# A two-layer convolution trunk on one core: each silu as one table function, the GLU's sigmoid from a tanh

## The chip, the cores and the metric

One core of a Trainium2 chip runs the kernel. Its engines work side by side, each through its own queue in order: TensorE (PE in the profile; PEld is its weight load), VectorE (DVE), ScalarE (ACT), GpSimd (POOL) and SyncE (SP), whose queue issues all transfers here. An engine that waits at an instruction holds up everything behind it in its queue. The metric is the device time of one execution in microseconds (us); lower is better.

## The reference, cut to what matters

Input x is 2048 tokens by 1024 channels in float32. Two mixers, each followed by a residual and a layer norm:

```python
cond = silu(c)                                 # scales, shifts and gates come from products with it
# layer 0 (mixer A)
a, g, z = split(u @ w_in + b_in, 3)
h = a * sigmoid(g)                             # the GLU
h = causal_depthwise_conv_31(h) + conv_b
h = silu(layer_norm_channels(h, ln_g, ln_b))
y = (h * silu(z)) @ w_out + b_out
# layer 1 (mixer B)
B, C, v, z = split(u @ w_in, 4)
y = (B * conv_3(C * v) * silu(z)) @ w_out
# both: u = x * (1 + scale) + shift;  x = layer_norm(alpha * x + gate * y)
```

silu(t) is t times sigmoid(t), and sigmoid(t) equals 0.5 * tanh(t / 2) + 0.5.

## The kernel before

Tokens go in four quarters q of 512, channels in eight blocks e of 128. A tile of 128x512 holds one block of channels (partitions) for one quarter. Every float32 operand of a product is split in a high part (a cast on ScalarE, L118 and L150) and a low part (a subtraction, mostly on GpSimd, L120 and L151), and a product is three matmuls: high with high, high with low, low with high. One output block of an input product is 24 matmuls (8 blocks of u, three each).

In layer A, `a_in` makes blocks a, g, z for each e (tiles `pi`, one PSUM bank each). `gated_a` (L446 to L451) copies a with its bias to `av`, makes `sg`, the sigmoid of g, and GpSimd multiplies them to `h`. `conv_a` then runs 31 taps in two chains, `pca` and `pcb`, which VectorE adds up (L409); ScalarE starts them (L397 `pcb`, L398 `acc`). There are two PSUM banks for the chains, so that `pcb` of block e can start only when block e-1 is done. `silu_z_a` copies z to `zv`, makes `sz`, its sigmoid, and GpSimd multiplies them (L458 to L461); the result goes to DRAM and comes back later as `zz`, in two buffers.

`a_norm` brings the conv's outputs `acc` to norm: for each e two VectorE rows with the broadcast statistics (L546, L547), then on ScalarE `v` (the scaled and shifted value, L550) and `sv` (its sigmoid, L552), then on VectorE v*sv (L555) and v*zz (L556), then the split to `ga` (cast on ScalarE, low part on GpSimd). `mixer_out` multiplies `ga` by W_out (tiles `wo`, loaded in pairs of blocks, two raw buffers) into four banks `po`, one per 128 tokens, for two halves of the output channels.

In layer B, `gated_b` takes the four blocks `pq`; for z it makes the sigmoid `szb` (L606, ScalarE) and multiplies it by z, read from its PSUM bank, on VectorE (L607). The banks of `pi`, `pq` and `po` come from one pool of four (tag mm), so a `po` bank is the bank of an earlier `pi` or `pq`, and comes free when the last reader of that is done.

`prep` loads blocks of x (`xk`, two buffers), transposes them on TensorE into `ptx` and makes `u`.

The program is written as generators that are woven together by a table of numbers (`SCH`); the order in each engine's queue is then set by a list scheduler with a timing model of its own. Any change of an instruction can thus move others in all queues.

Of the kernel before, what the change touches and what calls it, by code (L numbers as in the profile page):

```python
# [9 lines left out]
F32 = mybir.dt.float32  # L10
F32R = mybir.dt.float32r
AF = mybir.ActivationFunctionType
ALU = mybir.AluOpType
# [3 lines left out]
P = 128  # L17
# [21 lines left out]
def hybrid_trunk(ctx, tc, x, c, ada_w, ada_b, a_w_in, a_b_in, a_conv_w, a_conv_b,  # L39
# [16 lines left out]
    # ------------------------------------------------------------ constants  # L56
# [48 lines left out]
    nc.scalar.activation(cond, col["c"], AF.Sigmoid)  # L105
    nc.vector.tensor_tensor(cond, cond, col["c"], op=ALU.mult)
# [5 lines left out]
    # ------------------------------------------------------------ helpers  # L112
    def weight(src, name, tags=MAIN):
        """A piece of a weight matrix as two float32r parts."""
# [15 lines left out]
    def products(pss, ws, acts):  # L130
        """One or more output blocks, the shared activations outermost."""
# [30 lines left out]
    def prep_k(q, l, k, src, su, bu, tag="xk"):  # L162
        """One block of channels of u, transposed, as two parts."""
# [26 lines left out]
    def ada_sum(l, m, h, res, shared=0):  # L190
        """Products of the condition with half a chunk of ada_w, not yet summed over partitions.

        The last shared ones are summed apart, by other engines.
        """
# [29 lines left out]
    def modulation_b():  # L224
        """Scale and bias of u of the second layer, its input being the first one's bare norm."""
# [21 lines left out]
    def fold_gate(l, w_out, scaled=None):  # L247
        """W_out with the gate of its output channels (over alpha); scaled is a row to take it too."""
# [27 lines left out]
    def mixer_out(q, l, gs, residual, finish, last=False):  # L276
        """r = residual + gated output product, rows in token order, then the norm."""
# [52 lines left out]
    # ------------------------------------------------------------ layer A  # L330
# [50 lines left out]
    in_order[0] = False  # L381
    todo = deque()
# [3 lines left out]
    def conv_a(q, e, h, accs):  # L386
        """Queues two interleaved chains of taps, so that no step waits for the one before it."""
# [55 lines left out]
    def gated_a(q, e, pa, pg, accs):  # L443
        bias = lambda m: col["b_in"][:, m * K + e:m * K + e + 1]
        av = st("ta", [P, T], f"av{q}_{e}")
        nc.scalar.activation(av, pa, AF.Identity, bias=bias(0))  # L446
        sg = st("ta", [P, T], f"sg{q}_{e}")
        nc.scalar.activation(sg, pg, AF.Sigmoid, bias=bias(1))
# [6 lines left out]
    def silu_z_a(q, e, pz):  # L455
        bz = col["b_in"][:, 2 * K + e:2 * K + e + 1]
        zv = st("ta", [P, T], f"zv{q}_{e}")
        nc.scalar.activation(zv, pz, AF.Identity, bias=bz)  # L458
        sz = st("ta", [P, T], f"sz{q}_{e}")
        nc.scalar.activation(sz, pz, AF.Sigmoid, bias=bz)  # L460
        nc.gpsimd.tensor_tensor(zv, zv, sz, op=ALU.mult)  # L461
        nc.sync.dma_start(z_dram[q, e], zv)
# [273 lines left out]
```

## Time and profile before

| What | Value |
|---|---|
| Median of 3 runs | 1782.88 us (1782.02 to 1783.66) |
| Profiled execution: span from first to last instruction | 1780.3 us (no other time of it is listed) |
| PE, DVE, POOL, ACT busy | 94%, 78%, 65%, 37% of the span |
| Mean granted TensorE clock | 0.978 of full speed |

The span is 2.6 us under the median; this is taken as what lies around it. Busy shares are means over stages with different limits.

### The profile page before, as it was taken

What the parts mean: (1) busy time and instruction counts of PE and PEld (TensorE: products, weight loads), DVE (VectorE), ACT (ScalarE), POOL (GpSimd) and SP (SyncE); (2) the same over time, 40 slices, a digit from 0 to 9 for tenths busy, and PEclk for the clock granted to TensorE, in tenths of its full rate; (3) what the DMA queues carried; (4) which work ended last, traced back from release to release, by engine and by line L of the source; (5) the groups of instructions that cost most, each with busy time, mean ns of one, the idle gap of its engine ahead of it and who ended that gap; (6) DMA issues with size and microseconds to landing.
All of it is one profiled execution on the core that took longest, in us unless ns stands there. A gap on an engine that the chain in (4) does not pass through costs nothing.

```text
span 1780.3 us, 20731 instructions
## 1 busy us (share of the span) xinstructions
PE 1675.2 (94%) x7468; PEld 1373.0 (77%) x7468; DVE 1383.5 (78%) x1811; ACT 654.4 (37%) x852; POOL 1157.2 (65%) x742
## 2 busy tenths in 40 slices
PE   6997998899999999999999799999999979999997
PEld 4775787678787787888888687888888868888886
DVE  7999999999996846899995926499996756354464
ACT  2443535545221543344422433243432424222221
POOL 3696857887665867766654857666654666664444
PEclk9998999899999999999999899999999989999999
DMA  9874334676653454533433454443333335443342
GB/s 250 269 242 154 101 118 154 227 229 201 219 176 103 152 191 164 182 114 107 116 87 94 142 166 172 160 130 113 90 107 103 133 107 201 128 144 95 95 142 83
DMA packets 332055, 265.29 MB, mean 149 GB/s; under 512 B 10536, under 2 KB 289456, under 8 KB 331952
## 3 DMA queue, kind: packets, MB, share of 16 engines
q1 hardware_dynamic: 331952, 263.96, 47.3%
q8 instruction: 59, 0.97, 0.2%
q14 instruction: 44, 0.36, 0.1%
HBM read 230.36 MB, written 33.55 MB: 148 GB/s over the span
## 4 chain that ended last, share of the span: by engine, by line
PE 62%; DVE 24%; issue 5%; POOL 4%; DMA 3%; SPq 1%; ACT 1%; POOLq 0%; DVEq 0%; ACTq 0%
PE pq L141 8%; PE pq L139 8%; PE pq L140 8%; PE pi L140 7%; PE pi L141 7%; PE pi L139 7%; DVE pca L409 5%; PE po L311 5%; PE po L313 5%; PE po L312 5%; DVE pcb L409 4%; DVE cc L611 2%; DVE ada L219 1%; DVE v L555 1%; POOL wb_lo L120 1%
## 5 line engine op out<-in xcount | busy, mean ns | idle before, releaser
L120 POOL TENSOR_TENSOR wb_lo<-wb_raw,wb_hi 128x1024 fp32r<-128x1024 f32 x128 | 311.6, 2437 | 213.6 <-ACT wb_hi L118 184.7
L409 DVE SCALAR_TENSOR_TENSOR pca<-h,cols,pca 128x512 f32<-128x512 f32 x440 | 328.3, 746 | 1.3
L409 DVE SCALAR_TENSOR_TENSOR pcb<-h,cols,pcb 128x512 f32<-128x512 f32 x416 | 310.3, 746 | 22.4 <-ACT pcb L397 22.2
L120 POOL TENSOR_TENSOR wi_lo<-wi_raw,wi_hi 128x1024 fp32r<-128x1024 f32 x96 | 234.3, 2442 | 133.8 <-ACT wi_hi L118 121.0
L118 ACT CAST wb_hi<-wb_raw 128x1024 fp32r<-128x1024 f32 x128 | 134.4, 1051 | 365.6 <-PE pq L140 176.8
L120 POOL TENSOR_TENSOR wo_lo<-wo_raw,wo_hi 128x1024 fp32r<-128x1024 f32 (+1 forms) x65 | 164.8, 2538 | 77.2 <-ACT wo_hi L118 59.7
L118 ACT CAST wi_hi<-wi_raw 128x1024 fp32r<-128x1024 f32 x96 | 100.6, 1048 | 211.1 <-PE pi L140 105.6
L320 DVE TENSOR_TENSOR r<-po,r 128x512 f32<-128x512 f32 x64 | 43.3, 681 | 169.8 <-PE po L313 169.6
L118 ACT CAST wo_hi<-wo_raw 128x1024 fp32r<-128x1024 f32 (+1 forms) x65 | 67.0, 1033 | 117.3 <-PE po L313 62.2
L611 DVE SCALAR_TENSOR_TENSOR cc<-hb,cols,cc 128x512 f32<-128x512 f32 x64 | 87.2, 1363 | 0.8
L602 DVE TENSOR_TENSOR hb<-pq,cv 128x512 f32<-128x512 f32 x32 | 22.0, 686 | 68.6 <-PE pq L141 65.1
L409 DVE SCALAR_TENSOR_TENSOR pca<-h,cols,acc 128x512 f32<-128x512 f32 x32 | 51.7, 1617 | 2.4 <-ACT acc L398 2.4
L141 PE MATMUL pq<-u_0h,wb_lo 128*128 128x512 f32 x128 | 50.7, 396 | 1.9 <-POOL wb_lo L120 1.9
L139 PE MATMUL pq<-u_0h,wb_hi 128*128 128x512 f32 x128 | 50.7, 396 | 1.6 <-ACT wb_hi L118 1.6
L139 PE MATMUL pi<-u_0h,wi_hi 128*128 128x512 f32 x96 | 39.2, 409 | 13.8 <-ACT wi_hi L118 12.6
L613 DVE TENSOR_TENSOR cc<-cc,szb 128x512 f32<-128x512 f32 x32 | 51.5, 1608 | 0.5
L141 PE MATMUL pq<-u_2h,wb_lo 128*128 128x512 f32 x128 | 50.9, 398 | 0.0
L140 PE MATMUL pq<-u_4l,wb_hi 128*128 128x512 f32 x128 | 50.3, 393 | 0.0
L140 PE MATMUL pq<-u_6l,wb_hi 128*128 128x512 f32 x128 | 50.2, 392 | 0.0
L140 PE MATMUL pq<-u_0l,wb_hi 128*128 128x512 f32 x128 | 50.2, 392 | 0.0
L140 PE MATMUL pq<-u_7l,wb_hi 128*128 128x512 f32 x128 | 50.1, 392 | 0.0
L141 PE MATMUL pq<-u_4h,wb_lo 128*128 128x512 f32 x128 | 50.1, 392 | 0.0
(376 smaller groups left out, 5228.8 us busy)
## 6 DMA issues: line engine op xcount, KB each, us to landing
wb_raw<-in_b_w_in_dram SPq DMA_DIRECT2D x128, 512.0 KB
wi_raw<-in_a_w_in_dram SPq DMA_DIRECT2D x96, 512.0 KB
wo_raw<-w_dram SPq DMA_DIRECT2D x63, 512.0 KB
adaw<-in_ada_w_dram SPq DMA_DIRECT2D x60, 256.0 KB
adak<-in_ada_w_dram SPq DMA_DIRECT2D x32, 256.0 KB
xk<-in_x_dram SPq DMA_DIRECT2D x32, 256.0 KB
z_dram<-zv SPq DMA_DIRECT2D x32, 256.0 KB
zz<-z_dram SPq DMA_DIRECT2D x32, 256.0 KB
```

Source lines behind the costliest of these rows:

```text
L118: nc.scalar.copy(hi, raw)
L120: nc.gpsimd.tensor_tensor(lo, raw, hi.bitcast(F32), op=ALU.subtract)
L139: nc.tensor.matmul(ps, hi[k], ah, start=(k == 0), stop=False)
L140: nc.tensor.matmul(ps, hi[k], al, start=False, stop=False)
L141: mm = nc.tensor.matmul(ps, lo[k], ah, start=False, stop=(k == K - 1))
L311: nc.tensor.matmul(pss[t], gh[:, sl], hi, start=(k == 0), stop=False)
L312: nc.tensor.matmul(pss[t], gh[:, sl], lo, start=False, stop=False)
L313: nc.tensor.matmul(pss[t], gl[:, sl], hi, start=False, stop=(k == K - 1))
L320: nc.vector.tensor_tensor(r, pss[t], r, op=ALU.add)
L409: nc.vector.scalar_tensor_tensor(out=ts[dst], in0=h[:, k:k + T], scalar=wa_col(k, e), in1=ts[src], op0=ALU.mult, op1=ALU.add)
L611: nc.vector.scalar_tensor_tensor(out=cc, in0=hb[:, k:k + T], scalar=wbc(k), in1=cc, op0=ALU.mult, op1=ALU.add)
L613: nc.vector.tensor_tensor(cc, cc, sz, op=ALU.mult)
```

## The change

Every silu becomes one ScalarE instruction with the function Silu: for the condition, for z of layer A, after layer A's norm, and for z of layer B. Three copies-or-sigmoids per place become one, and the products go: 32 on GpSimd (L461), 64 and one small one on VectorE (L555, L607, L106). In the GLU the sigmoid becomes a tanh with scale 0.5 and a halved bias, and one more ScalarE instruction, `sg*0.5 + 0.5`. Two small constants are added. ScalarE's queue holds one table load, at the condition's function, before and after; in the changed queue Silu and Tanh follow each other 56 times.

```diff
-    nc.scalar.activation(cond, col["c"], AF.Sigmoid)
-    nc.vector.tensor_tensor(cond, cond, col["c"], op=ALU.mult)
+    nc.scalar.activation(cond, col["c"], AF.Silu)
...
+    half_bg = const.tile([P, K], F32, name="half_bg")
+    nc.vector.tensor_scalar(half_bg, col["b_in"][:, K:2 * K], 0.5, None, op0=ALU.mult)
+    half_col = const.tile([P, 1], F32, name="half_col")
+    nc.vector.memset(half_col, 0.5)
...
         sg = st("ta", [P, T], f"sg{q}_{e}")
-        nc.scalar.activation(sg, pg, AF.Sigmoid, bias=bias(1))
+        nc.scalar.activation(sg, pg, AF.Tanh, scale=0.5, bias=half_bg[:, e:e + 1])
+        nc.scalar.activation(sg, sg, AF.Identity, scale=0.5, bias=half_col)
...
-        nc.scalar.activation(zv, pz, AF.Identity, bias=bz)
-        sz = st("ta", [P, T], f"sz{q}_{e}")
-        nc.scalar.activation(sz, pz, AF.Sigmoid, bias=bz)
-        nc.gpsimd.tensor_tensor(zv, zv, sz, op=ALU.mult)
+        nc.scalar.activation(zv, pz, AF.Silu, bias=bz)
         nc.sync.dma_start(z_dram[q, e], zv)
...
-            nc.scalar.activation(v, pt, AF.Identity, scale=g_, bias=b_)
-            sv = st("tv", [P, T], f"sv{q}_{e}")
-            nc.scalar.activation(sv, pt, AF.Sigmoid, scale=g_, bias=b_)
+            nc.scalar.activation(v, pt, AF.Silu, scale=g_, bias=b_)
             zz = st("zz", [P, T], f"zz{q}_{e}")
             nc.sync.dma_start(zz, z_dram[q, e])
-            nc.vector.tensor_tensor(v, v, sv, op=ALU.mult)
             nc.vector.tensor_tensor(v, v, zz, op=ALU.mult)
...
-        nc.scalar.activation(sz, pss[2], AF.Sigmoid)
-        nc.vector.tensor_tensor(sz, pss[2], sz, op=ALU.mult)
+        nc.scalar.activation(sz, pss[2], AF.Silu)
```

The queues change in order too. In the rows below the first number behind a tile's name is the block e (for `wi` and `pi` e and which of a, g, z), and for `xk`, `ptx` and `u` the quarter and the block; a trailing longer number is only the program's count of tiles. The line numbers of the changed kernel are one lower up to the GLU, and a few higher behind it.

ScalarE, first quarter of layer A, around the start of block 3's chain `pcb`, before:

```order
L118 CAST wi_5_2_hi<-wi_5_2_raw 128x1024
L397 ACTIVATE pcb_3_1128<-h_3_1030,cols_397 128x512
L446 ACTIVATE av_5_1315<-pi_5_0_1248,cols_199 128x512
L118 CAST wi_6_0_hi<-wi_6_0_raw 128x1024
L448 ACTIVATE sg_5_1317<-pi_5_1_1290,cols_199 128x512
L118 CAST wi_6_1_hi<-wi_6_1_raw 128x1024
```

The same place of the same queue in the changed kernel:

```order
L117 CAST wi_6_0_hi<-wi_6_0_raw 128x1024
L449 ACTIVATE av_5_1308<-pi_5_0_1241,cols_198 128x512
L400 ACTIVATE pcb_3_1123<-h_3_1028,cols_396 128x512
L117 CAST wi_6_1_hi<-wi_6_1_raw 128x1024
L452 ACTIVATE sg_5_1310<-pi_5_1_1283,half_bg 128x512
L453 ACTIVATE sg_5_1310<-sg_5_1310,half_col 128x512
```

The cast of the weights of block 6's a now stands ahead of `pcb` of block 3, where it stood behind it.

ScalarE, norm of the third quarter (the second in which `po` follows blocks `pq` of layer B), around the sigmoid `szb` of block 6, before:

```order
L150 CAST ga_4h<-v_4_8103 128x512
L552 ACTIVATE sv_6_8133<-acc_6_7233,cols_199 128x512
L118 CAST wo_2_0_4_hi<-wo_2_0_4_raw 128x1024
L150 CAST ga_5h<-v_5_8117 128x512
L606 ACTIVATE szb_6_8331<-pq_6_3_8306 128x512
L550 ACTIVATE v_7_8145<-acc_7_7304,cols_199 128x512
L150 CAST ga_6h<-v_6_8131 128x512
L552 ACTIVATE sv_7_8147<-acc_7_7304,cols_199 128x512
L150 CAST ga_7h<-v_7_8145 128x512
```

The same place in the changed kernel:

```order
L149 CAST ga_5h<-v_5_7996 128x512
L552 ACTIVATE v_7_8018<-acc_7_7202,cols_198 128x512
L149 CAST ga_6h<-v_6_8007 128x512
L149 CAST ga_7h<-v_7_8018 128x512
L117 CAST wo_2_0_4_hi<-wo_2_0_4_raw 128x1024
L149 CAST gb_5h<-cc_5_8060 128x512
L605 ACTIVATE szb_6_8200<-pq_6_3_8175 128x512
```

`szb` of block 6, now the silu and the last reader of its bank, stands behind the casts of the whole norm, where the sigmoid stood behind `ga_5h`.

TensorE, first quarter of layer A, where the first blocks of the second quarter are transposed, before:

```order
L139 MATMUL pi_3_1_1001<-u_0_0h,wi_3_1_hi 128x512
L140 MATMUL pi_3_1_1001<-u_0_0l,wi_3_1_hi 128x512
L169 MATMUL ptx_1_0_1668<-ident,xk_1_0_1666 128x128 x4
L169 MATMUL ptx_1_1_1681<-ident,xk_1_1_1679 128x128
L141 MATMUL pi_3_0_959<-u_0_0h,wi_3_0_lo 128x512
```

TensorE in the changed kernel, at the end of that quarter:

```order
L138 MATMUL pi_7_2_1618<-u_0_7h,wi_7_2_hi 128x512
L139 MATMUL pi_7_2_1618<-u_0_7l,wi_7_2_hi 128x512
L140 MATMUL pi_7_2_1618<-u_0_7h,wi_7_2_lo 128x512
L168 MATMUL ptx_1_0_1655<-ident,xk_1_0_1653 128x128 x3
L168 MATMUL ptx_1_1_1668<-ident,xk_1_1_1666 128x128 x4
L168 MATMUL ptx_1_2_1681<-ident,xk_1_2_1679 128x128 x4
L168 MATMUL ptx_1_3_1694<-ident,xk_1_3_1692 128x128 x4
L138 MATMUL pi_0_2_1757<-u_1_0h,wi_0_2_hi 128x512
```

The transposes of blocks 0 to 3 of the second quarter, which lay within blocks 3 to 5 of the first, now stand together behind its last product and ahead of the second quarter's first.

## Rows read from the trace of the kernel before

**Rows 1.** The page, its head and part 1: busy time and share of the span.

```profile
span 1780.3 us, 20731 instructions
PE 1675.2 (94%) x7468; PEld 1373.0 (77%) x7468; DVE 1383.5 (78%) x1811; ACT 654.4 (37%) x852; POOL 1157.2 (65%) x742
```

**Rows 2.** Waits of PE: who waited for whom, us in total, times, longest.

```profile
PE po L311 <- DVE szb L607: 21.6, 3, 10.7
```

**Rows 3.** Timeline, first quarter: start, duration, instruction, idle before and its releaser.

```profile
125.19 14.17 DVE L409 SCALAR_TENSOR_TENSOR pca<-h,cols,acc 128x512 f32<-128x512 f32 x1
153.21 0.69 ACT L397 ACTIVATE pcb<-h,cols 128x512 f32<-128x512 f32 x1 [16.76 <-DVE acc L409]
155.49 0.79 PE L139 MATMUL pi<-u_0h,wi_hi 128*128 128x512 f32 x1 [11.78 <-ACT wi_hi L118]
```

**Rows 4.** Windows: us, busy PE, PEld, DVE, ACT, POOL, clock, DMA share, GB/s.

```profile
118.00:145.00 27.00, 25.71 (x116) 20.94 (x114) 26.96 (x21) 9.78 (x13) 26.27 (x20) 1.00 0.88 276
986.40:1022.96 36.56, 25.77 (x107) 20.61 (x106) 32.98 (x28) 17.33 (x24) 31.66 (x18) 0.86 0.41 142
319.40:326.20 6.80, 6.05 (x14) 4.79 (x15) 4.59 (x3) 3.17 (x5) 5.52 (x5) 0.50 0.29 101
1008.90:1019.20 10.30, 3.87 (x9) 3.10 (x10) 9.15 (x8) 3.19 (x5) 6.35 (x6) 0.50 0.17 62
```

**Rows 5.** Groups by line: shapes, count, busy us and mean ns, idle before.

```profile
L552 ACT ACTIVATE sv<-acc,cols 128x512 f32<-128x512 f32 x32 | 25.9, 810 | 12.8 <-DVE v L555 12.8
L402 ACT ACTIVATE part<-h,cols 128x512 f32<-128x512 f32 x8 | 5.7, 714 | 0.0
...
L461 POOL TENSOR_TENSOR zv<-zv,sz 128x512 f32<-128x512 f32 x32 | 42.4, 1325 | 2.0 <-ACT sz L460 2.0
...
L555 DVE TENSOR_TENSOR v<-v,sv 128x512 f32<-128x512 f32 x32 | 44.3, 1384 | 1.4 <-ACT sv L552 1.4
L607 DVE TENSOR_TENSOR szb<-pq,szb 128x512 f32<-128x512 f32 x32 | 21.8, 682 | 16.7 <-ACT szb L606 14.0 <-DMA wb_raw<-in_b_w_in_dram 2.7
L409 DVE SCALAR_TENSOR_TENSOR pca<-h,cols,acc 128x512 f32<-128x512 f32 x32 | 51.7, 1617 | 2.4 <-ACT acc L398 2.4
```

**Rows 6.** Timeline of PE, norm of the first quarter: its three waits for `ga`.

```profile
298.17 0.50 PE L311 MATMUL po<-wo_hi,ga_0h 128*128 128x512 f32 x1 [2.30 <-ACT ga_0h L150]
307.40 1.19 PE L313 MATMUL po<-wo_hi,ga_1l 128*128 128x512 f32 x4 [2.57 <-POOL ga_1l L151]
320.15 2.07 PE L313 MATMUL po<-wo_hi,ga_4l 128*128 128x512 f32 x4 [4.29 <-POOL ga_4l L151]
```

**Rows 7.** Timeline, norm of the third quarter.

```profile
986.39 1.64 POOL L151 TENSOR_TENSOR ga_0l<-v,ga_0h 128x512 fp32r<-128x512 f32 x1 [0.66 <-ACT ga_0h L150]
1006.00 0.59 ACT L606 ACTIVATE szb<-pq 128x512 f32<-128x512 f32 x1
1014.60 0.68 DVE L607 TENSOR_TENSOR szb<-pq,szb 128x512 f32<-128x512 f32 x1
1015.33 0.79 PE L311 MATMUL po<-wo_hi,ga_0h 128*128 128x512 f32 x1 [10.65 <-DVE szb L607]
1017.43 0.69 DVE L556 TENSOR_TENSOR v<-v,zz 128x512 f32<-128x512 f32 x1
1020.33 2.63 POOL L120 TENSOR_TENSOR wo_lo<-wo_raw,wo_hi 128x1024 fp32r<-128x1024 f32 x1 [0.18 <-ACT wo_hi L118]
1030.29 1.44 DVE L320 TENSOR_TENSOR r<-po,r 128x512 f32<-128x512 f32 x2 [9.60 <-PE po L313]
```

**Rows 8.** Timeline of PE: the same wait in the norms of the second and fourth quarter.

```profile
609.21 0.53 PE L311 MATMUL po<-wo_hi,ga_0h 128*128 128x512 f32 x1 [2.63 <-DVE hb L602]
1437.64 0.79 PE L311 MATMUL po<-wo_hi,ga_0h 128*128 128x512 f32 x1 [9.43 <-DVE szb L607]
```

**Rows 9.** Timeline of PE: a wait for a freshly issued load of `xk`.

```profile
400.76 0.63 PE L169 MATMUL ptx<-ident,xk 128*128 128x128 f32 x4 [3.98 <-DMA xk<-n_dram]
```

**Rows 10.** Groups by line of ACT: the table load.

```profile
L105 ACT ACT_TABLE_LOAD x1 | 1.3, 1283 | 0.7 <-PEq L722 0.7
```

## Prediction

> **What bounds the kernel now.** The page's first part comes first: TensorE is busy 94% of the span, no other engine over 78% [rows 1]. So most of the time is matmuls that the change leaves alone, and what can be won lies in the 105 us in which TensorE is idle (1780.3 less 1675.2), and in the slow clock behind such idling. The waits of PE say who ends them, and the largest sum is a PSUM bank that the first matmuls of `po` wait for until VectorE has multiplied `szb`, 21.6 us in three waits [rows 2]. The timeline shows each stall. I read five places off it.
>
> In the first quarter PE stands 11.8 us for a weight cast. Behind that is a chain: ScalarE waits 16.8 us at `pcb` for VectorE's conv, with the cast queued behind it, and VectorE is late since one tap, whose two tile operands (`h` and `acc`) both lie in SBUF, took 14.17 us [rows 3]. The 32 instructions of this kind average 1.62 us; without this one they would average 1.21 (51.7 less 14.2, by 31) [rows 5]. In that window GpSimd worked 26.3 of 27 us [rows 4]. I read it as VectorE locked out by GpSimd's back-to-back reads of SBUF.
>
> The other four places are the layer A norms, one per quarter. In the first, PE waits three times for `ga`, 9.2 us in all [rows 6]. In the third it stands 10.65 us until VectorE's `szb` product at 1014.60 frees the fourth bank, though ScalarE had that sigmoid done at 1006.59; VectorE's queue held the product behind products of the norm [rows 7]. The fourth quarter repeats it with 9.4 us, and the second waits 2.6 us [rows 8].
>
> Two of these stalls are followed by stretches at a granted clock of 0.50, which is 1.2 of 2.4 GHz, after PE had idled [rows 4]. Half of PE's busy time there is loss: 3.0 us in the first norm (6.05 busy), 1.9 in the third (3.87).
>
> **The change part by part.** VectorE loses 32 products v*sv at 1.38 us and 32 `szb` products at 0.68, 66.1 us in all; GpSimd loses 32 products `zv`, 42.4 us [rows 5]. ScalarE loses 64 functions and gains 32 affine steps of `sg`. No row shows Silu, so I bound it: it can't be cheaper than nothing, and the same form with a sigmoid takes 0.81 [rows 5]; twice that would mean that it took two passes. I take 0.81. The affine step (SBUF to SBUF, one column operand) is nearest to `part`, 0.71 [rows 5]. It lies on the way from g to `h`, and so to the first taps; the cover is VectorE's backlog of taps, which is older. Without that cover it would cost 32 x 0.71 = 23 us. The bank of g is free after the tanh, not after the affine step, so PE doesn't wait for it. The condition's missing product and the two constants are three small instructions at VectorE's start and middle; I cost them at nothing, and the loads that fill the start hide them.
>
> *First quarter.* With the `zv` products gone (two in that window, 2.65 of GpSimd's 26.3 us), GpSimd no longer runs without a gap, and VectorE should get its turn sooner. Besides, `pcb` of block 3 now stands behind the cast for the next weight block, so a late conv holds PE one output block later. I take the stall as gone: 11.8 us, and 1.9 for the clock (estimated as after the third norm's stall). But the transposes of the second quarter now stand together behind the first quarter's last product. `xk` has two buffers, so blocks 2 and 3 can only be loaded once 0 and 1 are transposed, and PE must wait for that load. The nearest row is a wait for a fresh load of 3.98 us [rows 9]. The lower bound is 0, since the last product might end late anyway, the upper one two such waits, 8 us. I take 4.0, and 1.9 more for the clock. What was queued there before, one block within other products, cost nothing that PE's waits name. Net: 13.7 - 5.9 = 7.8 us.
>
> *Norms.* Take the third. VectorE's last v*zz ends at 1018.1; less eight products of 1.38 it ends at 1007.0. `szb` of block 6 now stands on ScalarE behind the norm's last cast, so the bank comes free only then: four ScalarE instructions of about 0.8 more, 1010, against 1015.3. So the wait moves to ScalarE and gets shorter. What is late next is GpSimd, which makes the low parts of `ga` and `wo`: from 986.39 to 1022.96 (the last `wo_lo` of that half) it worked 31.7 of 36.6 us [rows 4, 7]. It has the same work there after the change. If all its 4.9 us of waits go, it ends at 1018.1. PE needs that `wo_lo` for the last two of eight blocks: from 1015.3 it worked off the last 63 of the half's 96 matmuls (3 for each of 8 blocks and 4 banks) until 1030.3 [rows 7], so 24 take 38% of 15.0 less 1.9, 5.0 us, which ends at 1023.1: 7.2 us saved of the 12.6 at stake (10.65 and 1.9). The bounds are 0 and 12.6. I carry this share, 0.57, to the other norms: first, 9.2 + 3.0 = 12.2 gives 7.0; second, 2.6 gives 1.5; fourth, 9.4 + 1.9 = 11.3 gives 6.4. Together 22.1 us.
>
> *Elsewhere* I count nothing: layer B's `szb` products leave VectorE where PE is busy without a gap, and the work that hides them is PE's own.
>
> Sum: 7.8 + 22.1 = 29.9 us off the profiled span of 1780.3, which gives 1750.4; the median of the runs lies 2.6 above the span, so 1753.0.
>
> On the lock-out the trace and a page differ. The tap stood 14.17 us in a window in which no GpSimd instruction that a row shows takes over 2.63 [rows 3, 7]. The Trainium skill (SBUF — State Buffer, section "Who interferes with whom") says that a VectorE instruction with two SBUF inputs contends with a GpSimd instruction that reads SBUF, and that whoever comes first holds the port for its whole instruction. By that a wait would be one instruction long, at most 2.6 us, the stall would have another cause that may stay, and the sum would be 22.1 - 5.9 = 16.2 us, 1766.7. The row shows the contention and a longer wait; I follow the row.
>
> **The rivals.**
> A. *The first quarter's stall stays*, at this place or another: GpSimd is still near full there, and the order of its queue has changed. Against it: fewer instructions, and the moved cast. Then 13.7 is not won: 1766.7.
> B. *The norms give little*: GpSimd's low parts or the `zz` loads (two buffers, each refilled after a v*zz) take over as the pace. For it: GpSimd's 31.7 of 36.6 us. If only 5 of the 22.1 come: 1770.1.
> C. *Everything comes back*: stakes of 13.7, 12.2, 2.6, 12.6 and 11.3 us and no new wait, 52.4: 1730.5.
> D. *Slower by lock-outs*: each block's first tap (32 of them) can be caught as that one was, and each hit costs PE 13.7. Two hits bring 1780.4, no change; from three on the kernel is slower, 1794.1. For it: longest runs of GpSimd products without a break are set by a new order. Against it: one hit in 32 before.
> E. *Slower by table loads*: if Silu and Tanh could not share a table, 56 alternations at 1.28 us [rows 10] would add 72 us to ScalarE; it decides from 23 of them on PE's path, and with half there the time is 1789. The queue of the changed kernel holds one load, as before, which speaks against it. The Trainium skill (ScalarE: Activation LUTs, section "Table sets: the hidden batching unit") gives the rule that each switch to another set costs a load, some 2.7 us with its drain, and doesn't list Silu in a set; by that figure the 56 would be 150 us.
>
> **How the numbers follow.** Forecast 0.48; C 0.15; A 0.18; B 0.07; D with two hits 0.04, with three or more 0.05; E 0.03. The measurement can tell about 0.2%, 3.6 us, from no change. Faster: 0.48 + 0.15 + 0.18 + 0.07 = 0.88; the same 0.04; slower 0.08. The time is that of the forecast, 1753.0. The range reaches down to C and up past A and B's start, 1730 to 1772, which leaves out D, E and part of B. The forecast's own range is 1742 to 1764.
>
> **What would show it.** In the changed profile: no tap over 5 us and no `pcb` wait over 8 in the first quarter; PE waiting for `xk` at its end, some 4 us; `po`'s waits for `szb` gone from VectorE and standing at ScalarE's `szb` or at `wo_lo`, under 5 us each; VectorE busy near 1300 us (1383.5 less 66 and the lock-out), GpSimd near 1115; one table load; Silu at 0.81. Wrong would make it: a new long wait of ScalarE at `pcb`, or Silu at 1.6.

## The result and the profile after

| Kernel | Median | Runs |
|---|---|---|
| before, beside it | 1783.27 us | 1782.02 to 1789.16 |
| changed | 1741.74 us | 1740.85 to 1743.19 |

The ratio is 0.9752 (95% interval 0.9729 to 0.9776): 2.5% faster, about 44 us of 1783. The forecast was 1753.0 in a range of 1730 to 1772, so sign and range held and the gain was larger than forecast (29.9).

The page's first part after, to be read against [rows 1]:

```profile
span 1740.0 us, 20572 instructions
PE 1669.4 (96%) x7468; PEld 1371.9 (79%) x7468; DVE 1313.7 (76%) x1748; ACT 636.1 (37%) x820; POOL 1114.6 (64%) x710
```

PE has the same 7468 matmuls, and its idle time fell from 105.1 us (1780.3 less 1675.2) to 70.6. The other 5.8 us are busy time. The mean granted clock rose from 0.978 to 0.982, which goes with that; how much of the 5.8 us it makes is not shown.

The waits of PE after (who waited for whom: us in total, times, longest), against [rows 2]:

```profile
PE ptx L168 <- ACT uf L170: 7.5, 2, 7.0
...
PE po L311 <- POOL wo_lo L119: 6.3, 4, 3.2
...
PE pm L235 <- DVE ada L218: 5.6, 1, 5.6
...
PE po L310 <- ACT szb L605: 2.2, 1, 2.2
```

The 21.6 us for VectorE's `szb` are gone. What is left of them stands where the prediction put it: 2.2 us at ScalarE's `szb`, 6.3 in four waits at GpSimd's `wo_lo`. Two lines are new: the first, and the one at `pm`, for which the kernel before doesn't wait.

The timeline of the first quarter after, where [rows 3] had the stall:

```profile
122.33 1.12 DVE L412 SCALAR_TENSOR_TENSOR pca<-h,cols,acc 128x512 f32<-128x512 f32 x1
137.31 0.69 ACT L400 ACTIVATE pcb<-h,cols 128x512 f32<-128x512 f32 x1
...
181.78 0.69 ACT L400 ACTIVATE pcb<-h,cols 128x512 f32<-128x512 f32 x1
182.41 1.03 ACT L117 CAST wi_hi<-wi_raw 128x1024 fp32r<-128x1024 f32 x1
183.34 0.68 ACT L463 ACTIVATE zv<-pi,cols 128x512 f32<-128x512 f32 x1
183.93 0.77 ACT L170 ACTIVATE uf<-ptx,mod 128x512 f32<-128x512 f32 x1
184.75 1.12 PE L168 MATMUL ptx<-ident,xk 128*128 128x128 f32 x4 [6.96 <-ACT uf L170]
```

The tap that took 14.17 us takes 1.12, and `pcb` of block 3 starts at 137.31 without a wait (153.21 before). At the quarter's end PE waits 6.96 us at the transposes that now stand together, and the releaser is ScalarE: `uf`, the reader of the first `ptx` bank, stands in its queue behind `pcb` of block 5, a weight cast and `zv`.

Each kernel has one traced execution, so whether the long tap comes in every execution of the kernel before is not on record. In the twelve traces of whole kernels in this study, with 32 taps of that form each, two stand out: this one and one of 5.86 us further below. The next longest takes 3.00.

Windows after, columns as in [rows 4]; the first is the stretch of the long tap, the second the one behind the new wait:

```profile
118.00:145.00 27.00, 27.00 (x121) 22.31 (x120) 26.77 (x40) 12.60 (x17) 26.31 (x21) 1.00 0.79 252
182.20:189.00 6.80, 3.75 (x12) 2.62 (x12) 6.73 (x10) 5.13 (x8) 6.49 (x5) 0.50 0.58 181
```

GpSimd is as full as it was, 26.31 of 27 us against 26.27. That speaks against the prediction's reason for the first quarter (that GpSimd would no longer run without a gap), though the stall is gone.

Groups by line after (shapes, count, busy us and mean ns, idle before), against [rows 5]:

```profile
L552 ACT ACTIVATE v<-acc,cols 128x512 f32<-128x512 f32 x32 | 25.8, 814 | 18.5 <-DVE acc L549 18.5
L453 ACT ACTIVATE sg<-sg,half_col 128x512 f32<-128x512 f32 x32 | 23.2, 724 | 0.7
```

Silu costs what the sigmoid did (814 ns against 810), and the affine step the 0.71 assumed.

PE in the four norms after. The first norm has no wait for `ga` any more ([rows 6] had three); the first line is its new wait, for a sum `ada` on VectorE that feeds layer B's modulation:

```profile
309.51 0.56 PE L235 MATMUL pm<-ones,ada 128*128 128x1 f32 x2 [5.63 <-DVE ada L218]
594.32 0.50 PE L311 MATMUL po<-wo_lo,ga_4h 128*128 128x512 f32 x1 [1.31 <-POOL wo_lo L119]
983.51 0.51 PE L310 MATMUL po<-wo_hi,ga_0h 128*128 128x512 f32 x1 [2.18 <-ACT szb L605]
1401.85 0.80 PE L311 MATMUL po<-wo_lo,ga_4h 128*128 128x512 f32 x1 [3.20 <-POOL wo_lo L119]
```

The last three answer 2.63, 10.65 and 9.43 us in [rows 7, 8].

**Where the time came from.** I cut both spans at GpSimd's `sb` of each norm (its last statistic) and at VectorE's first `r<-po` of that norm's second half. Windows after, the nine stretches:

```profile
0.00:265.25 265.25, 236.60 (x1055) 191.20 (x1056) 249.99 (x417) 110.32 (x147) 177.18 (x130) 0.97 0.64 192
265.25:342.77 77.52, 70.27 (x295) 57.33 (x294) 68.65 (x89) 41.09 (x57) 68.54 (x43) 0.93 0.66 223
342.77:552.50 209.73, 199.30 (x909) 163.19 (x908) 193.11 (x263) 73.55 (x95) 142.98 (x99) 0.96 0.60 190
552.50:625.77 73.27, 71.96 (x330) 59.12 (x329) 32.34 (x43) 29.69 (x38) 56.62 (x30) 1.00 0.50 162
625.77:945.96 320.19, 317.34 (x1429) 262.39 (x1428) 264.62 (x345) 119.41 (x154) 192.77 (x124) 0.99 0.42 129
945.96:1023.33 77.37, 74.63 (x334) 61.02 (x333) 44.05 (x45) 28.83 (x37) 57.46 (x32) 0.98 0.49 154
1023.33:1356.51 333.18, 331.93 (x1501) 274.69 (x1500) 262.04 (x348) 123.94 (x159) 198.18 (x128) 1.00 0.41 127
1356.51:1434.57 78.06, 73.46 (x314) 59.62 (x313) 41.60 (x46) 26.09 (x33) 56.13 (x31) 0.96 0.42 136
1434.57:1740.00 305.43, 293.92 (x1313) 243.36 (x1311) 157.32 (x156) 83.18 (x101) 164.70 (x100) 0.99 0.40 128
```

The cuts don't hold the same matmuls before and after: in the first quarter 1055 stand where 1082 stood, so 27 have moved behind the cut. A matmul takes 0.22 us (317.34 by 1429 in the fifth row), and with it each difference can be set right, as an estimate:

| Stretch | Length before, after | PE's instructions before, after | Difference, at equal work | Forecast |
|---|---|---|---|---|
| first quarter | 278.90, 265.25 | 1082, 1055 | -13.7, -7.7 | -7.8 |
| first norm | 82.91, 77.52 | 290, 295 | -5.4, -6.5 | -7.0 |
| to the second norm | 210.59, 209.73 | 887, 909 | -0.9, -5.7 | 0 |
| second norm | 76.61, 73.27 | 326, 330 | -3.3, -4.2 | -1.5 |
| to the third norm | 319.07, 320.19 | 1433, 1429 | +1.1, +2.0 | 0 |
| third norm | 84.86, 77.37 | 330, 334 | -7.5, -8.4 | -7.2 |
| to the fourth norm | 337.45, 333.18 | 1505, 1501 | -4.3, -3.4 | 0 |
| fourth norm | 83.12, 78.06 | 314, 314 | -5.1, -5.1 | -6.4 |
| rest | 306.79, 305.43 | 1313, 1313 | -1.4, -1.4 | 0 |

The sum is -40.3 of span. Two terms are off by more than 2 us: the second norm (2.7), and the stretches between the norms, counted as nothing, which gave 8.5. The first three rows together hold 2259 instructions of PE in both kernels, so their sum of -19.9 (forecast -14.8) needs no such estimate; how it is shared among the three does.

### The profile page after: what moved, and what is told of

Read it like the earlier page. It is cut to its first block, busy times and chain, and to the rows that moved or that the text cites. A ratio compares the mean times of both kernels' runs of the same rounds, so it can differ in the third digit from the quotient of the medians.

```text
span 1740.0 us, 20572 instructions
## 1 busy us (share of the span) xinstructions
PE 1669.4 (96%) x7468; PEld 1371.9 (79%) x7468; DVE 1313.7 (76%) x1748; ACT 636.1 (37%) x820; POOL 1114.6 (64%) x710
## 4 chain that ended last, share of the span: by engine, by line
PE 72%; DVE 11%; POOL 5%; DMA 5%; issue 4%; ACT 2%; SPq 1%; POOLq 0%; DVEq 0%; ACTq 0%
PE pq L138 11%; PE pq L139 11%; PE pq L140 11%; PE pi L139 7%; PE pi L140 7%; PE pi L138 7%; PE po L311 5%; PE po L312 5%; PE po L310 5%; POOL wi_lo L119 1%; DVE pca L412 1%; DVE v L555 1%; DVE pcb L412 1%; PE ptx L168 1%; DVE acc L548 1%
## 5 line engine op out<-in xcount | busy, mean ns | idle before, releaser
L609 DVE SCALAR_TENSOR_TENSOR cc<-hb,cols,cc 128x512 f32<-128x512 f32 x64 | 95.3, 1489 | 1.1
L611 DVE TENSOR_TENSOR cc<-cc,szb 128x512 f32<-128x512 f32 x32 | 55.7, 1740 | 15.8 <-ACT szb L605 15.2
L168 PE MATMUL ptx<-ident,xk 128*128 128x128 f32 x256 | 40.3, 290 | 16.7 <-ACT uf L170 7.5
L168 PEld LDWEIGHTS ptx<-ident,xk 128*128 128x128 f32 x256 | 32.9, 150 | 24.4 <-ACT uf L170 8.1
L218 DVE SCALAR_TENSOR_TENSOR ada<-adaw,cond,ada 128x512 f32<-128x512 f32 x32 | 48.7, 1522 | 2.5 <-DMA adaw<-in_ada_w_dram 2.1
L138 PE MATMUL pq<-u_7h,wb_hi 128*128 128x512 f32 x128 | 50.3, 400 | 0.0
L139 PE MATMUL pq<-u_2l,wb_hi 128*128 128x512 f32 x128 | 50.1, 392 | 0.0
L138 PE MATMUL pq<-u_1h,wb_hi 128*128 128x512 f32 x128 | 50.1, 391 | 0.0
```

Source lines behind the costliest of these rows:

```text
L138: nc.tensor.matmul(ps, hi[k], ah, start=(k == 0), stop=False)
L139: nc.tensor.matmul(ps, hi[k], al, start=False, stop=False)
L168: nc.tensor.transpose(pt[:, t * P:(t + 1) * P], xk[:, t, :], ident)
L609: nc.vector.scalar_tensor_tensor(out=cc, in0=hb[:, k:k + T], scalar=wbc(k), in1=cc, op0=ALU.mult, op1=ALU.add)
L611: nc.vector.tensor_tensor(cc, cc, sz, op=ALU.mult)
```

## The experiments

Gains are compared as ratios to the kernel before, run beside each; a difference of 0.001 is 1.8 us. Each ratio has an interval of about +-0.0026, so two of them differ for certain only from about 0.004, some 7 us. Every edit also moves the order of the queues, so a run shows its product together with a new order. What order alone can do is seen in the run with early transposes: 8 us.

| Kernel | Median us | Ratio to before | 95% interval |
|---|---|---|---|
| changed | 1741.74 | 0.9752 | 0.9729 to 0.9776 |
| z's product on GpSimd again | 1746.39 | 0.9781 | 0.9754 to 0.9809 |
| v's product on VectorE again | 1764.59 | 0.9882 | 0.9858 to 0.9907 |
| the same in the first norm alone | 1751.38 | 0.9802 | 0.9779 to 0.9824 |
| `szb`'s product on VectorE again | 1758.22 | 0.9851 | 0.9825 to 0.9877 |
| Sigmoid in the GLU | 1737.22 | 0.9729 | 0.9702 to 0.9757 |
| no affine step | 1735.15 | 0.9726 | 0.9702 to 0.9751 |
| transposes early | 1733.67 | 0.9709 | 0.9678 to 0.9740 |
| Sigmoid and transposes early | 1738.02 | 0.9730 | 0.9701 to 0.9760 |
| transposes early, one tap off VectorE | 1748.83 | 0.9775 | 0.9753 to 0.9796 |
| before with copies on GpSimd | 1783.19 | 0.9991 | 0.9969 to 1.0013 |

### z's product back on GpSimd

```diff
-        nc.scalar.activation(zv, pz, AF.Silu, bias=bz)
+        nc.scalar.activation(zv, pz, AF.Identity, bias=bz)
+        sz = st("ta", [P, T], f"sz{q}_{e}")
+        nc.scalar.activation(sz, pz, AF.Silu, bias=bz)
+        nc.gpsimd.tensor_tensor(zv, zv, sz, op=ALU.mult)
```

> The changed kernel with layer A's z as before in its instructions: a copy with bias to `zv`, a second function for `sz`, and the product on GpSimd (32 x 1.33 us). The second function is Silu, so that no table is loaded; what comes out there is z times silu(z). My theory (GpSimd's freed queue ended VectorE's lock-out and made the first quarter shorter, 13.6 us by the stages): that quarter loses most of it again, 8 to 13.6 us, and the time is 1750 to 1755; a tap of over 5 us or a wait of ScalarE at `pcb` of over 8 us is back in the first quarter. Rival (the place of the casts ahead of `pcb` alone did it, or VectorE's lighter load): 1741.7 within 3.6, and the lock-out may be back without holding PE.

0.0029 above the changed kernel, 5 us, between the two expectations and not resolved. In its queues the casts stand behind `pcb` of block 3 and the transposes lie within the first quarter, as before the change. Its first quarter ends at 266.33, 12.6 us earlier than before (11.0 at equal work, 1075 instructions of PE). Its timeline has the long tap again, shorter, on VectorE, and the GpSimd copy in which it ended:

```profile
123.45 5.86 DVE L412 SCALAR_TENSOR_TENSOR pca<-h,cols,acc 128x512 f32<-128x512 f32 x1
...
128.68 0.69 POOL L455 COPY h<-halo 128x30 f32<-128x30 f32 x1
```

The copy takes 0.69 us where such copies take about 0.21 (the median); I read it as VectorE's tap getting its turn there. The tap of 14.17 us before ended in the same way, at 139.36, in a copy that took 0.75 from 138.67. PE's wait for the cast is 2.07 us. So my theory fell in its number: with the 32 products back and GpSimd as busy as before (26.11 of 27 us), most of the stall stays away. As far as one trace tells, a freed GpSimd is not what shortened the first quarter. That the length of the wait depends on how the two queues meet is my reading, and not shown.

### v's product back on VectorE

```diff
-            nc.scalar.activation(v, pt, AF.Silu, scale=g_, bias=b_)
+            nc.scalar.activation(v, pt, AF.Identity, scale=g_, bias=b_)
+            sv = st("tv", [P, T], f"sv{q}_{e}")
+            nc.scalar.activation(sv, pt, AF.Silu, scale=g_, bias=b_)
...
+            nc.vector.tensor_tensor(v, v, sv, op=ALU.mult)
             nc.vector.tensor_tensor(v, v, zz, op=ALU.mult)
```

> The changed kernel with the norm's v in the instructions of before: an affine copy, a second function for `sv`, and the product on VectorE (32 x 1.38 us). The second function is Silu, so that no table is loaded; what comes out is v times silu(v). My theory (the eight products per norm, 11 us of VectorE, set the end of the norm and with it the start of `po`): the norms, 21.3 us shorter by the stages, lose 10 to 21 of it, and the time is 1752 to 1763, the first quarter staying short. Rival (what mattered is only that the `szb` bank is freed by ScalarE, not VectorE): within 3.6 of 1741.7.

0.0130 above, 23 us: the theory's range, and slightly beyond. But the norms don't lose alike. PE's wait at the start of `po` in the third norm is 4.08 us, on ScalarE's `szb`, against 2.18 in the changed kernel and 10.65 before. Almost half of the 23 us goes in the first norm:

```profile
266.40:363.41 97.01, 81.24 (x335) 65.36 (x333) 87.94 (x108) 54.23 (x76) 78.29 (x49) 0.88 0.61 207
```

That stretch took 77.52 us in the changed kernel, at 295 instructions of PE; at equal work (40 less) it is still 10.7 longer.

### v's product back in the first norm alone

The same edit under `if q == 0`.

> The changed kernel with the product v*sv back on VectorE in the first norm alone (8 x 1.38 us; v times silu(v) comes out there, in the first quarter). My theory now: from 60 us to the statistics of the second norm VectorE is busy 94 to 96% and sets the length of the stretch (462 of 492 us in the changed kernel, 479 of 506 with all v*sv back); so these eight products alone cost 11 us or somewhat more of the 22.9 that all 32 cost: 1752 to 1757, and the stretch ends about 13 us later. Rival (each norm loses its part, as the sum of the prediction had it; a quarter of 22.9): 1746 to 1748, the first norm alone being longer and the time coming back behind it.

0.0050 above, 9 us, between the theory (10 to 15) and the rival (4 to 6), nearer to the theory but not resolved between them: in the profiled executions 9.2 of the 23.0 us that all four norms cost. PE's waits in this norm are 3.28 for ScalarE's `sg`, 4.51 for `ga_4l` and 5.10 and 3.50 for `ada`, a sum on VectorE that only stands in its queue behind the norm. Of these the changed kernel has one, the 5.63 for `ada`.

### `szb`'s product back on VectorE

```diff
         nc.scalar.activation(sz, pss[2], AF.Silu)
+        nc.vector.tensor_tensor(sz, pss[2], sz, op=ALU.mult)
```

> The changed kernel with the product of `szb` back on VectorE (32 x 0.68 us), which reads the bank of z last; what comes out is z times silu(z). My theory (third and fourth norm waited for this product because it stood behind v*sv and v*zz; v*sv is still gone): the wait of `po` for VectorE's `szb` is back in these two norms at a few us each, together 3 to 8, and the 5.5 us gained between the norms go too as far as they came from VectorE's load in layer B: 1745 to 1755. Rival (v*sv alone made the gain): within 3.6 of 1741.7, and `po` waits under 3 us for `szb`.

0.0099 above, 18 us, more than my 3 to 13. (Its profiled execution, 1763.36, is 5.1 above the median.) PE in the third and fourth norm, and between them:

```profile
999.78 0.79 PE L310 MATMUL po<-wo_hi,ga_0h 128*128 128x512 f32 x1 [3.79 <-DVE szb L606]
1070.37 0.50 PE L310 MATMUL po<-wo_hi,gb_0h 128*128 128x512 f32 x1 [1.53 <-DVE szb L606]
1076.69 0.50 PE L310 MATMUL po<-wo_hi,gb_0h 128*128 128x512 f32 x1 [2.17 <-DVE cc L614]
1416.67 0.79 PE L310 MATMUL po<-wo_hi,ga_0h 128*128 128x512 f32 x1 [3.81 <-DVE szb L606]
```

The norms' waits are 3.8 each: this product alone does not make 10.65, nor do the v products alone (4.08). Taking either part away ends most of that stall. The two stalls at `gb_0h` are new here against the changed kernel, which has one of 1.25. They are those of the kernel before, which also has the third line, a wait of the transposes `pl` for VectorE's statistics shortly before the second norm:

```profile
1085.74 0.50 PE L311 MATMUL po<-wo_hi,gb_0h 128*128 128x512 f32 x1 [1.54 <-DVE szb L607]
1092.06 0.50 PE L311 MATMUL po<-wo_hi,gb_0h 128*128 128x512 f32 x1 [2.18 <-DVE cc L615]
550.62 1.11 PE L509 MATMUL pl<-ident,acc 128*128 128x128 f32 x4 [2.74 <-DVE s L512]
```

The changed kernel doesn't wait at `pl`; with the product back it does:

```profile
542.19 1.12 PE L511 MATMUL pl<-ident,acc 128*128 128x128 f32 x4 [2.74 <-DVE s L514]
```

Windows of this run for the stretches to the second and to the fourth norm:

```profile
344.19:563.41 219.22, 201.58 (x909) 163.90 (x908) 199.24 (x269) 72.77 (x95) 141.24 (x98) 0.95 0.57 181
1037.56:1375.54 337.98, 334.28 (x1505) 276.24 (x1504) 265.74 (x354) 123.72 (x159) 196.38 (x128) 0.99 0.41 126
```

The changed kernel takes 209.73 (909 instructions of PE) and 333.18 (1501) for them, the kernel before 210.59 (887) and 337.45 (1505). So with layer B's products back on VectorE these stretches are 9.5 and, at equal work, 3.9 us longer than in the changed kernel, where the prediction counted nothing. The 9.5 is more than the change had gained there (5.7), so not all of it is the product.

### Sigmoid in the GLU, with its table loads

```diff
-        nc.scalar.activation(sg, pg, AF.Tanh, scale=0.5, bias=half_bg[:, e:e + 1])
-        nc.scalar.activation(sg, sg, AF.Identity, scale=0.5, bias=half_col)
+        nc.scalar.activation(sg, pg, AF.Sigmoid, bias=bias(1))
```

> The changed kernel with the GLU's sigmoid as one function Sigmoid in place of tanh and the affine step; the values are the reference's. Its queue on ScalarE holds 55 table loads in place of one. By the row of one load in the trace before, 1.28 us each, that is 69 us of ScalarE, less 32 affine steps. My theory (rival E of the prediction, in a kernel that has the loads): ScalarE is busy 37% of the time and the loads lie in layer A; a third of them on PE's path or in front of a release, some 23 us: 1765. Rival 1 (ScalarE's slack hides them): within 3.6 of 1741.7. Rival 2 (each on the path, with the engine drained around it): 1810 and over.

Groups by line of ScalarE; 52 of the 55 loads stand at the GLU's sigmoid and at z's silu:

```profile
L452 ACT ACT_TABLE_LOAD x27 | 34.6, 1283 | 1.9 <-issue 1.5
...
L462 ACT ACT_TABLE_LOAD x25 | 32.1, 1283 | 0.4
```

The ratio is 0.0023 below that of the changed kernel: not resolved, and certainly no loss of 23 us. My theory fell, and the time is even a little under rival 1's: 69 us more of loads on ScalarE, with 23 us of affine steps gone, cost nothing that can be measured. One part of that is a different order: the first transposes of the second quarter lie within the first quarter again, fewer stand behind it, and PE waits 1.94 us there instead of 6.96.

### No affine step

```diff
-        nc.scalar.activation(sg, sg, AF.Identity, scale=0.5, bias=half_col)
```

> The changed kernel without the affine step of the GLU (h is a times tanh(g/2), so 32 ScalarE instructions of 0.72 us are gone; what is left out is the halving and the added half). The prediction's term (the step costs nothing, since VectorE's older taps cover it): within 3.6 of 1741.7. Rival (the step lies in front of `h` and of the first taps, and in front of casts in ScalarE's queue): up to 23 us less, 1719 to 1738. With the run that has Sigmoid there, which also lacks the step and has 54 more table loads and took 1737.2, the difference of the two is the price of these loads.

0.0026 below, 5 us, not resolved; the median lies in the rival's range, far from its 23 us. (The profiled execution took 1730.0 us, 5 under the median, so no length of a stage is read from it.) Against the Sigmoid run the difference is 0.0003: 54 loads cost nothing beyond the noise. Here too the transposes are woven into the quarter again, and PE waits 0.52 us in their place, so that what the step costs can't be told from what the order gives.

### Transposes of the second quarter early

```diff
-    prep(0, 1)
+    with tc.high_priority(offset=BOOST):
+        prep(0, 1)
```

> The changed kernel with the preparation of the second quarter given a higher priority, so that its transposes are woven into blocks 3 and later of the first quarter instead of standing together behind it. My theory (that lump cost the changed kernel the 7.0 us wait of PE at `ptx` and a stretch at half clock behind it, 3.4 us of the 6.8): 6 to 10 us less than the changed kernel, 1732 to 1736. Rival (the same casts and low parts now press on ScalarE and GpSimd in a quarter in which they are full, and the time comes back as waits for weights): within 3.6 of 1741.7.

1733.67 us, 0.0043 below, 8 us, as the theory had it. It has the lowest median of the study, but is not resolved from the runs with Sigmoid and without the affine step. No wait at `ptx` for ScalarE is left in the first quarter, which is now

```profile
0.00:262.66 262.66, 242.90 (x1073) 196.43 (x1074) 249.44 (x414) 112.08 (x150) 179.60 (x130) 0.99 0.66 197
```

with 18 instructions more in 2.6 us less than in the changed kernel.

### Both together

The edits of the last run and of the one with Sigmoid.

> Both together: Sigmoid in the GLU (55 table loads, the reference's values) and the transposes of the second quarter early. The run with Sigmoid stalled PE only 1.9 us at these transposes, so if the two do not disturb each other: 1732 to 1737. Rival (the loads hurt where ScalarE must also make `u` of the second quarter): 1742 or more.

0.0021 above the run before it, inside the noise, and 1738.02 is just over the expected range. The gains don't show as a sum: with Sigmoid the transposes had hardly been in the way (1.94 us).

### Copies in GpSimd's run, in the kernel before

```diff
+        spare = const.tile([P, 30], F32, name=f"spare{l}")
...
                 tc.keep_in_program_order(nc.gpsimd.tensor_tensor(w, w, grow, op=ALU.mult))
+                if l == 0:
+                    tc.keep_in_program_order(nc.gpsimd.tensor_copy(spare, w[:, :30]))
```

> The kernel before, with 16 small GpSimd copies (128x30) added, one for each product `wf` of the first fold, which the scheduler places between GpSimd's products of the first quarter; nothing is taken away, and ScalarE's casts stand behind `pcb` of block 3 as before. My theory now (after the run with z back on GpSimd, where the long tap was 5.86 us and ended during a GpSimd copy, as the one of 14.17 did before): a tap with two operands in SBUF that is caught waits through GpSimd's products until a copy comes, so more copies mean short waits. The first quarter's tap is under 6 us, PE's stall of 11.78 under 3, and the time 8 to 13.7 us less than before: 1771 to 1776. Rival (the long tap has another cause, or GpSimd's added work costs as much): the tap stays near 14 us, and the time is within 3.6 of 1785.

Half right. No tap of the convolution takes over 2.93 us, PE's stall of 11.78 is gone, and the first quarter ends at 264.95, 13.9 us earlier than before (8.2 at equal work: 1056 instructions). That the copies did it is not shown, since nine of the other traces have no longer tap either, without them. Yet the time is that of the kernel before, 0.9991. The first norm takes part of it back, 2.9 us at equal work (93.10 us and 323 instructions against 82.91 and 290). PE's waits there:

```profile
294.47 0.50 PE L314 MATMUL po<-wo_hi,ga_0h 128*128 128x512 f32 x1 [3.23 <-ACT sg L451]
310.78 2.08 PE L316 MATMUL po<-wo_hi,ga_4l 128*128 128x512 f32 x4 [4.68 <-POOL ga_4l L151]
...
331.78 0.80 PE L314 MATMUL po<-wo_hi,ga_0h 128*128 128x512 f32 x1 [5.54 <-DVE r L323]
```

Between the norm's first row on VectorE and its first `r`, VectorE's queue holds 26 taps into the two chains, where that of the kernel before holds 17: the scheduler had woven it anew. The changed kernel holds 24 there, but without the eight products v*sv. From 60 us to the second norm's `sb`, before and with the copies (windows of the two kernels, one row each):

```profile
60.00:572.40 512.40, 467.90 (x2072) 379.98 (x2071) 493.36 (x651) 211.26 (x284) 383.82 (x260) 0.96 0.57 181
```

```profile
60.00:573.10 513.10, 467.94 (x2070) 379.65 (x2069) 488.52 (x651) 212.05 (x284) 388.46 (x277) 0.96 0.57 180
```

VectorE, the third busy time, is busy 96 and 95% of it, and the end of PE's stall bought nothing by the end of the stretch. That is no rule: the run with early transposes ends PE's wait of 6.96 us in the same stretch with the same work on VectorE (462.5 us, and 462.1 in the changed kernel), and takes 485.7 us for it against 492.5.

### One tap of the second quarter off VectorE

```diff
-        lead = 1 + (SCH["c0"] if q == 0 else SCH["cq"])
+        lead = 1 + (SCH["c0"] if q < 2 else SCH["cq"])
```

on top of the early transposes.

> The run with early transposes, and in the second quarter's convolution one more tap of each block made off VectorE as in the first quarter (ScalarE makes `part`, GpSimd adds it: 8 x 0.71 and 8 x 1.3 us; VectorE loses 8 x 0.75 = 6.0 us). My theory (VectorE paces the stretch to the second norm): 3 to 6 us less than without it, 1728 to 1731. Rival (GpSimd's low parts or PE pace it, and VectorE's load is only a symptom): no change, 1733.7 within 3.6, or slower by GpSimd's 10 us, up to 1740.

My theory failed: 0.0066 above the run without it, 12 us slower, beyond the rival's 1740. The stretch from 60 us, first with the early transposes, then with the tap moved as well:

```profile
60.00:545.70 485.70, 461.49 (x2072) 376.06 (x2071) 462.52 (x637) 207.31 (x276) 366.16 (x244) 0.98 0.60 190
```

```profile
60.00:559.20 499.20, 468.92 (x2072) 380.60 (x2071) 464.94 (x628) 212.96 (x284) 376.27 (x253) 0.96 0.57 184
```

VectorE has nine instructions less and is busy 2.4 us longer, so others take longer; that this comes from GpSimd's 10 us more is likely and was not isolated. So the edit did not do what it was for. PE waits 6.15 us for `uf` at a transpose near 400 us. What would come of a lighter VectorE alone is not shown by it.

### The port by itself

Two programs that compute nothing of the reference, with VectorE's taps (`scalar_tensor_tensor`, 128x512) beside runs of GpSimd products:

```python
nc.gpsimd.tensor_tensor(g_i, src, zero, op=ALU.add)                 # 10 in a row, no break
nc.vector.scalar_tensor_tensor(out=acc, in0=v_in, scalar=col, in1=acc, op0=ALU.mult, op1=ALU.add)
```

> A program that computes nothing of the reference (the output is zeros): five phases, in each of which VectorE runs eight taps (scalar_tensor_tensor, 128x512) while GpSimd runs products. A: ten products 128x512, all operands in SBUF, without a break. B: the same ten with a copy of 128x30 after every second. C: ten scalings with one SBUF operand. D: six products of 128x1024. E: as A, but the taps' accumulator in PSUM. My theory (VectorE's tap with two SBUF operands is locked out for GpSimd's whole unbroken run, and a copy lets it in): in A one tap takes about 10 x 1.25 = 12 us, in B 2.5 to 3.5 us, in D some 14 us, in C and E no tap over 2.6. Rival (the wait is at most one GpSimd instruction, which is the rule in the Trainium skill, SBUF — State Buffer, section "Who interferes with whom"): no tap over 2.0 in A and B, none over 3.2 in D.

Timeline of VectorE: the first tap of phases A to D, and the seven that follow the first in A and E.

```profile
3.77 1.63 DVE L54 SCALAR_TENSOR_TENSOR accA<-vinA,col 128x512 f32<-128x512 f32 x1
5.44 11.63 DVE L54 SCALAR_TENSOR_TENSOR accA<-vinA,col,accA 128x512 f32<-128x512 f32 x7
...
21.42 1.63 DVE L54 SCALAR_TENSOR_TENSOR accB<-vinB,col 128x512 f32<-128x512 f32 x1
...
39.73 0.98 DVE L54 SCALAR_TENSOR_TENSOR accC<-vinC,col 128x512 f32<-128x512 f32 x1
...
57.79 2.71 DVE L54 SCALAR_TENSOR_TENSOR accD<-vinD,col 128x512 f32<-128x512 f32 x1
...
79.56 5.50 DVE L50 SCALAR_TENSOR_TENSOR bankE<-vinE,col,bankE 128x512 f32<-128x512 f32 x7
```

The rival holds. In A every tap takes 1.63 us, read as its own time and the rest of one GpSimd product; in D the first takes 2.71 beside products of twice the size; copies (B) change nothing; with one operand in PSUM (E) a tap takes 0.76. The Trainium skill (SBUF — State Buffer, section "SBUF: two separate sides") has the rule that whoever comes first holds the shared port for its whole instruction. The 1.63 and 2.71 us agree with it.

The second program copies the kernel's mix: two chains in PSUM, three taps per phase with two SBUF operands, GpSimd's `wf`, low parts and `av` products, each behind a semaphore.

> A second program that computes nothing of the reference (zeros): VectorE alternates the two chains of the kernel (accumulators in PSUM) and has three taps per phase with two operands in SBUF, while GpSimd runs the kernel's mix without a break, each product behind a semaphore of a transfer or of ScalarE: `wf` in place, low parts 128x1024, products of an `av`. Eight phases, 24 such taps. Theory (a wait of several GpSimd instructions, as 5.86 and 14.17 us in the kernels, comes from such mixes): at least one of the 24 takes over 3.5 us. Rival (one GpSimd instruction at most, as in the first such program, and the kernels' long taps need something that is not in here): none over 3.2 us.

None of its 24 such taps takes over 2.05 us. So two runs have a wait of one GpSimd instruction at most, and two kernels have one of 5.86 and 14.17 us. What these two have that the small programs lack stays open.

## Why the prediction was right, and where not

**First quarter, -7.8: right in size (-7.7 at equal work, an estimate), not shown in its reason, and in part luck.** The stall went, but GpSimd is as full as before (26.31 of 27 us), and with the products put back the stall stays small. The change ordered both queues anew; that this ended the stall is inferred from these runs. The cost on the other side was foreseen in its place and not in its releaser: not a load of `xk` (4.0) but ScalarE's queue in front of `uf` (6.96). The clock behind it cost 1.9 us (6.8 us at 0.50, the lower of its two levels, with PE busy 3.75), as estimated. The run with early transposes gives 8 us back and so shows that cost. What evened out most of the 3 us is another term that was not forecast: the waits for `wi_lo` in this quarter fell from 4.2 to 1.7 us.

**Norms.** Third: -8.4 against -7.2, and the chain is the one described; PE's wait went from VectorE to ScalarE's `szb` and GpSimd's `wo_lo`, each under 5 us. The undo runs show that v's and `szb`'s products were two causes, either of them enough to keep about 4 of the 10.65 us. Fourth: -5.1 against -6.4. First: -6.5 against -7.0, a good number by luck: all 9.2 us of waits for `ga` went, and not a share, but 5.63 for `ada` came, which the prediction did not have. It also left out a stretch at a clock of 0.51 behind the first of those waits (3.3 us busy from 298.9). Second: -4.2 against -1.5. Its stake was taken as the 2.63 us of one wait alone; behind that wait the trace of before has 3.4 us busy at a clock of 0.51 (609.6 to 613.0), 1.7 us of loss that was left out.

**Elsewhere, 0: the step that failed.** "Layer B's `szb` products leave VectorE where PE is busy without a gap": PE had gaps there, and I had not read them off the trace of before. They stand at `gb_0h` (1.54 and 2.18 us) and, with the conv of the second quarter beside layer B, at `pl` before the second norm (2.74 us). The 1.54 is even the third of the three waits in [rows 2], of which the prediction used two. With the product put back those gaps return to a hundredth of a microsecond, and the two stretches are 9.5 and 3.9 us longer with them. This term and the second norm make up the difference between 29.9 and 40.3.

**Rivals.** A (the stall stays), B (the norms give little) and D (lock-outs) did not come. C (everything comes back, 1730.5) did not come either, but 1741.74 lies just under the forecast's own range of 1742 to 1764, as near to C as to the forecast. E (table loads) did not apply, since one load is in the trace; had it applied it would have cost little here: 54 loads in the Sigmoid run cost nothing measurable, where E had a price of 1.28 us for half of them. The Trainium skill's rule by which each change of table set costs a load (ScalarE: Activation LUTs, section "Table sets: the hidden batching unit") holds in that run's rows. The rows have 1.28 us a load, 52 loads together have 2.3 us of idle time in front of them, and behind 53 of the 55 the next function starts within 0.02 us, so the 2.7 us a load of the Trainium skill are not seen here. That the loads set the time does not follow. By the rule of the Trainium skill on the port the stall's other cause might have stayed (1766.7). That rule is right in the two small programs, the stall went all the same, and its cause is open.

**Added up.** Undoing one part at a time costs 5 (z, not resolved), 23 (v) and 18 us (`szb`), 46 together against a gain of 44. So VectorE's 64 products, with the order that goes with them, made most of the gain; GpSimd's 32, on which the prediction hung a quarter of it, made little or nothing.

**What stays open:** what holds a tap for several GpSimd instructions, and whether it does so in every execution; how much of each undo run is the product and how much the order; and what share of the first quarter's gain would last without the rest, since the run with copies, which has that gain alone, gave it back under a new order of VectorE's queue.

## What to carry to other kernels

Before a saving is counted as nothing "because TensorE is busy there", list TensorE's short waits in that very stretch with their releasers: such stretches gave 8.5 of the 40.3 us here. Where one engine is busy 95% of a long stretch, don't count the end of another engine's stall in it as a term of its own without looking further: in one run it bought nothing, in another 6.8 us. Less work on the full engine (the products v*sv and `szb`) counted in every run that tested it. And count a table load by the slack of its engine: at 40% busy, ScalarE hid 54 of them.

## What the runs showed of the hardware that was not expected

- Silu and Tanh share a table (one load with 56 changes between them), Silu and Sigmoid don't (55 loads); a load takes 1.283 us each time.
- A tap with two SBUF operands beside an unbroken run of GpSimd products waits for one of them (1.63 us in all, 2.71 beside products twice as long). Twice in the twelve traces of whole kernels one took far longer (5.86 and 14.17 us) and ended in a small GpSimd copy, which then took 0.69 and 0.75 us instead of about 0.21.
- Beside GpSimd's scalings, which have one SBUF operand, such a tap took 0.98 us where beside products it took 1.63.
